# SwiGLU output products of three parts of four as seven block products for eight

## The chip, the cores and the metric

The kernel runs on one core of one Trainium2 chip. The metric is the device time of one execution in microseconds (us). Five engines are named: PE (TensorE) multiplies matrices and writes its sums into eight banks of PSUM; DVE (VectorE) and ACT (ScalarE) work element by element and read those banks; POOL (GpSimd) here issues transfers that add to what is in on-chip memory, and small copies; SP (SyncE) issues the plain transfers. Each engine takes its instructions in the order in which the program wrote them, and waits at one whose inputs are not there.

## The reference

Two layers of a decoder run over 544 tokens at once (512 of a prompt, 32 of eight samples), width 1024. Each layer has a SwiGLU feed-forward (FFN), a mixer and a second FFN, each added to the scaled input and normalised:

```python
def swiglu(x, w_in, w_out):
    g, u = jnp.split(x @ w_in, 2, axis=-1)
    return (jax.nn.silu(g) * u) @ w_out
...
x = layer_norm(ALPHA * x + 0.5 * swiglu(x, ffn1_w_in[layer], ffn1_w_out[layer]), ...)
```

`w_in` is 1024 x 5632 and `w_out` 2816 x 1024. There are four FFNs; the mixer of layer 0 is a retention with eight recurrent states of the samples per head, that of layer 1 a gated linear recurrence (RG-LRU). All in float32.

## The kernel before

**Precision and layout.** Activations lie transposed: 128 channels on the partitions, tokens along the row, in two halves of 272 tokens (`HF`). To multiply float32 values the kernel splits each operand into a high and a low part: ACT writes the high part (L314), DVE subtracts it from the source for the low part (L333), and a tile product is three matmuls (`mm3`, L372): high-high, high-low, low-high. `H`, the middle of the FFN, is 22 chunks of 128 channels; `Z` holds the sums that go to the normalisation; `X` is the split input.

**An FFN**, four times (`ffn`, L854), in this order: chunks 0 to 3 of H by plain products (the plain stage: 4 chunks, gate and up, two halves, 8 tiles, 3 matmuls: 384); then pairs of chunks (`pair`, L945), in which the two halves of tokens, the two halves of the 1024 inputs and the two chunks make 2 x 2 blocks, and seven block products stand for eight (Strassen and Winograd's way): 7 forms x 2 (gate, up) x 4 tiles x 3 = 168 matmuls. The forms of the weights (sums such as a21 + a22, called s1 to s4) are made by transfer: a block is loaded by SP (L489), another is added to it by POOL with an accumulating transfer (L477, `prev` and `more` in `use`, L416). The forms of X are made once per FFN (`sums`, L902). H is used in three parts, `PARTS = [(0, 8), (8, 16), (16, 22)]` (L36); after each part its product with `w_out` is done tile by tile (for 8 chunks: 8 outputs x 2 halves x 8 tiles x 3 = 384 matmuls), four outputs at a time (`gangs`), and DVE adds each bank to Z (`zev`, L699). With the last part the normalisation (`ln`, L621) begins.

**Supply of weights.** A unit is 128 x 1024 weights. It lands in one of 6 `raw` buffers (4 KB a partition; L48), is split by ACT and DVE (`split`, L447) into one of 6 `hl` buffers (8 KB; L49), and is freed by the last matmul that reads it. In the plain stage and in the RG-LRU two more hl buffers lie in unused working memory (`EXT`, L51, as `ext`); in pairs, output products and the retention there are none. A state of the retention keeps its raw buffer until the new state is stored (L515).

**Order.** Every instruction stream is written at build time by a small model of the engines (`Flow`): generators `yield` a time or an event, and are resumed when the modelled PE clock reaches it. Units are split in the order in which they were registered (`units`), and loaded in that order, with those that need an added block moved two places ahead (`order_loads`, `AHEAD`). The order of the instructions of each engine is thus fixed before the run; on the chip only semaphores wait.

## Time and profile before

| | |
|---|---|
| times of three runs | 2315.94, 2313.86, 2316.83 us; median 2315.94 |
| the profiled execution | 2316.85 us, of which the span (first to last instruction) 2315.1 |
| PE | 2273.5 us busy (98%), 17530 matmuls |
| DVE | 1540.3 us (67%) |
| ACT | 999.2 us (43%) |
| POOL | 143.7 us (6%) |
| transfers | 312.30 MB, mean 135 GB/s |
| mean granted PE clock | 0.992 |

Stages in us from the start of the span, by the outputs of PE and the loads: FFN 0 to 382, retention to 930, FFN to 1311, FFN to 1695, RG-LRU to 1937, FFN to the end. A row of the view by windows has: the stretch, its length, then the busy us (and the count of instructions) of PE, PEld (the loading of weights into PE), DVE, ACT and POOL, the granted clock of PE, the busy share of the 16 transfer engines, and GB/s. A row of the view by groups has: line, engine, operation, output <- inputs, shapes, count | busy us in total, mean ns of one | idle time of the engine before them and what ended it. A row of the timeline or of the chain of waits begins with the start and the length in us. An instruction's duration holds the way through its engine, so that two in a row overlap a little.

### The profile page before, as it was taken

To read this page: it belongs to the slowest core of one execution; us is meant where nothing else is said; L and a number is where in the kernel's file an instruction comes from. 1 tells how busy PE (TensorE), PEld (TensorE's weight loads), DVE (VectorE), ACT (ScalarE), POOL (GpSimd) and SP (SyncE) were. 2 spreads that over 40 slices of the span, in tenths; PEclk is the share of its full clock that TensorE was granted. 3 is DMA by queue.
4 is the path that set the end of the run, shared out by engine and by line. 5 is a ranking of instruction groups with operands and counts; after the bars stand their busy time and mean duration, and the time that the engine had idled before them with its cause. 6 is when DMAs were issued, how large, how long until landed. Compare 5 with 4: busy or idle time off the path is not lost.

```text
span 2315.1 us, 41946 instructions
## 1 busy us (share of the span) xinstructions
PE 2273.5 (98%) x17530; PEld 2230.4 (96%) x17530; DVE 1540.3 (67%) x2731; ACT 999.2 (43%) x1564; POOL 143.7 (6%) x195
## 2 busy tenths in 40 slices
PE   9999999999999999999999999999999999999997
PEld 9999998989899998999999899999989999999996
DVE  6646468776666677864746875564787678646467
ACT  5424244442434334542424453443458845424243
POOL 0011000000000000001100000101001000110000
PEclk9999999999999999999999999999999999999998
DMA  7666562153352543376756346665512232756651
GB/s 219 179 142 171 132 180 80 55 173 124 120 176 94 174 142 127 90 184 135 182 130 174 99 99 167 155 173 128 137 63 88 91 111 78 196 122 174 143 146 39
DMA packets 89486, 312.30 MB, mean 135 GB/s; under 512 B 9760, under 2 KB 13856, under 8 KB 89296
## 3 DMA queue, kind: packets, MB, share of 16 engines
q1 hardware_dynamic: 68016, 232.06, 30.5%
q0 software_dynamic: 21280, 77.56, 19.1%
q8 instruction: 137, 2.24, 0.4%
q14 instruction: 53, 0.43, 0.1%
HBM read 288.29 MB, written 21.29 MB: 134 GB/s over the span
## 4 chain that ended last, share of the span: by engine, by line
PE 91%; DVE 4%; issue 3%; ACT 1%; DMA 1%; SPq 0%; POOL 0%; ACTq 0%; POOLq 0%; DVEq 0%
PE bank L372 90%; PE bank L376 1%; DMA raw<-in_win 1%; DVE Z L333 1%; ACT ARF L314 0%; DVE ARF L342 0%; DVE Z L337 0%; DVE hl L333 0%; DVE ARF L333 0%; ACT hl L314 0%; DVE SM L351 0%; PE bank L380 0%; DVE ARF L337 0%; ACT Z L314 0%; DMA Z<-in_x 0%
## 5 line engine op out<-in xcount | busy, mean ns | idle before, releaser
L372 PE MATMUL bank<-BIG,hl 128*128 128x272 f32 x15096 | 1936.1, 290 | 16.7 <-ACT BIG L314 10.2
L372 PEld LDWEIGHTS bank<-BIG,hl 128*128 128x128 f32 x15096 | 1915.2, 189 | 28.9 <-ACT BIG L314 11.7
L333 DVE TENSOR_TENSOR hl<-raw,hl 128x1024 fp32r<-128x1024 f32 (+1 forms) x490 | 595.8, 1220 | 433.0 <-ACT hl L314 428.7
L314 ACT ACTIVATE hl<-raw 128x1024 fp32r<-128x1024 f32 (+1 forms) x490 | 511.8, 1054 | 661.3 <-PE bank L372 488.8
L314 ACT ACTIVATE BIG<-ARF 128x544 fp32r<-128x544 f32 (+11 forms) x234 | 131.1, 571 | 305.0 <-DVE ARF L337 219.5
L333 DVE TENSOR_TENSOR BIG<-ARF,BIG 128x544 fp32r<-128x544 f32 (+10 forms) x234 | 142.3, 618 | 110.2 <-ACT BIG L314 109.7
L477 POOL DMA_DIRECT2D raw<-in_win x144 | 125.2, 897 | 1395.6 <-DVE hl L333 749.0
L333 DVE TENSOR_TENSOR ARF<-bank,ARF 128x272 f32<-128x272 f32 (+3 forms) x460 | 187.0, 435 | 24.4 <-PE bank L372 16.6
L372 PE MATMUL bank<-BIG 128*128 128x272 f32 (+5 forms) x1172 | 193.7, 316 | 0.2 <-DVE ARF L342 0.2
L372 PEld LDWEIGHTS bank<-BIG 128*128 128x128 f32 (+3 forms) x1172 | 167.7, 188 | 13.7 <-DVE ARF L342 0.7
L372 PE MATMUL bank<-hl,BIG 128*128 128x256 f32 (+2 forms) x1024 | 145.7, 298 | 4.7 <-ACT BIG L314 4.2
L333 DVE TENSOR_TENSOR Z<-Z,bank 128x272 f32<-128x272 f32 (+1 forms) x230 | 110.5, 491 | 58.4 <-PE bank L372 53.7
L314 ACT ACTIVATE ARF<-bank 128x272 f32<-128x272 f32 (+5 forms) x278 | 108.8, 400 | 80.9 <-PE bank L372 51.3
L372 PEld LDWEIGHTS bank<-hl,BIG 128*128 128x128 f32 (+1 forms) x1024 | 126.4, 178 | 16.1 <-ACT BIG L314 4.6
L314 ACT ACTIVATE ARF<-Z 128x272 f32<-128x272 f32 (+1 forms) x86 | 39.3, 458 | 101.2 <-DVE Z L333 99.9
L333 DVE TENSOR_TENSOR ARF<-ARF 128x272 f32<-128x272 f32 (+1 forms) x146 | 61.2, 445 | 3.0 <-ACT ARF L314 1.4
L314 ACT ACTIVATE BIG<-Z,PR 128x272 fp32r<-128x272 f32 x80 | 40.8, 521 | 40.6 <-DVE Z L337 40.6
L314 ACT ACTIVATE ARF<-ARF 128x272 f32<-128x272 f32 x114 | 54.6, 492 | 3.6 <-DVE ARF L333 3.1
L337 DVE SCALAR_TENSOR_TENSOR Z<-Z,bank 128x272 f32<-128x272 f32 x80 | 33.5, 432 | 31.6 <-PE bank L372 31.4
L337 DVE SCALAR_TENSOR_TENSOR ARF<-ARF,PR 128x512 f32<-128x512 f32 (+1 forms) x92 | 40.5, 496 | 14.7 <-ACT ARF L314 14.7
L337 DVE SCALAR_TENSOR_TENSOR ARF<-ARF 128x272 f32<-128x272 f32 x84 | 46.7, 556 | 0.4
L337 DVE SCALAR_TENSOR_TENSOR raw<-raw,bank 128x512 f32<-128x512 f32 x64 | 40.9, 681 | 8.4 <-PE bank L372 8.3
(85 smaller groups left out, 653.2 us busy)
## 6 DMA issues: line engine op xcount, KB each, us to landing
raw<-in_win SPq DMA_DIRECT2D x173, 512.0 KB, 4.0
raw<-in_win POOLq DMA_DIRECT2D x144, 512.0 KB, 5.6
raw<-in_wout SPq DMA_DIRECT2D x88, 512.0 KB, 4.6
raw<-in_sret SPq DMA_DIRECT2D x32, 512.0 KB, 3.7
out_rets<-raw SPq DMA_DIRECT2D x32, 512.0 KB, 4.5
raw<-in_rwin_v SPq DMA_DIRECT2D x16, 512.0 KB, 3.6
raw<-in_rwin_kq SPq DMA_DIRECT2D x16, 512.0 KB, 3.7
raw<-in_rwin_g SPq DMA_DIRECT2D x16, 512.0 KB, 4.4
```

The lines of the kernel that those rows point to most:

```text
L314: nc.scalar.activation(out=out, in_=in_, func=func, scale=scale, **kw)
L333: nc.vector.tensor_tensor(out=out, in0=a, in1=b, op=op)
L337: nc.vector.scalar_tensor_tensor(out=out, in0=a, scalar=s, in1=b, op0=op0, op1=op1)
L372: nc.tensor.matmul(out, lhsT=a, rhs=b, start=start, stop=stop, skip_group_check=cont)
L376: nc.tensor.matmul(out, lhsT=a, rhs=b, start=start, stop=stop)
L477: nc.gpsimd.dma_start(out=u["raw"], in_=ap, accum_op=ALU.add)
```

## The change

The parts of H become `(0, 6), (6, 12), (12, 16), (16, 22)`. For the first three, the product with `w_out` is also done by seven block products: the 2 x 2 blocks are the two halves of tokens, the even and odd chunk of each pair of H, and two outputs out of four (`quad`: two per part, each 4 outputs). A quad of a part of 6 has 7 x 2 x 3 x 3 = 126 matmuls of 272 tokens, one of the part of 4 has 84. The fourth part stays tile by tile. For the quads the split forms of H (b11, b21, b22, n1, n3, nt, n4) are written by `put` and `mixed` at the end of each pair, and by `plain_forms` for chunks 0 to 3; their weights come in blocks of 768 or 512 columns, made into forms by the same loads and accumulating transfers. The seven forms, of pairs too, run in another order (`SEVEN`), and the banks of a quad are added to Z after every form. The order of the units changes with it. There are 5 raw and 5 hl buffers in place of 6 and 6; the memory goes into working memory that holds the forms of H, and the `ext` buffers become three in the plain stage and in the RG-LRU, and two in the last part of an FFN and in the retention. What is left out of the diff: the lines that go out of `pair`, the middle of `seven` (the three matmuls of each tile), the renamed `ext` arguments of the mixers, lengths of a unit in `split` and `pump`, and the signs in `sums`.

```diff
-PARTS = [(0, 8), (8, 16), (16, 22)]
-FH = 8
+PARTS = [(0, 6), (6, 12), (12, 16), (16, 22)]
+FH = 6
...
-N_RAW = 6
-N_HL = 6
-EXT = (10880, 12928, 8704, 13056)
+N_RAW = 5
+N_HL = 5
+EXT_R, EXT_S, EXT_M = (0, 1, 2), (3, 4, 5), (6, 7)
...
+    SEVEN = (("a11", 0), ("a12", 1), ("s2", 0), ("s3", 2), ("s1", 0), ("a22", 2), ("s4", 0))
...
+        res, last = [], None
+        for key, dram, n0, n in items:
+            blk = {f"a{r + 1}{c + 1}": dram[n0 + 2 * r + c] for r in range(2) for c in range(2)}
...
+            reg("s1", blk["a21"], more=blk["a22"])
+            if last:
+                last()
+            reg("a11", blk["a11"])
+            reg("a12", blk["a12"])
+            reg("s2", blk["a11"], prev=us["s1"])
+            reg("s3", blk["a21"], prev=us["a11"])
+            reg("a22", blk["a22"])
+            last = lambda reg=reg, blk=blk, us=us: reg("s4", blk["a12"], prev=us["s2"])
...
+    def seven(key, us, nk, moving, ev):
+        banks_of = {}
+        for form, bk in SEVEN:
+            u, mv = us[form], moving(form)
+            for i in range(2):
+                start = (bk, i) not in banks_of
+                if start:
+                    banks_of[bk, i] = acq_main()
+                else:
+                    fl.need(("rd", key, form, i))
...
+        def hforms(name, kk, n=1):
+            b = 6528 + 14 * HF * kk + ("b11", "b21", "b22", "n1", "n3", "nt", "n4").index(name) * 2 * HF
+            a = ARR[:, b:b + 2 * n * HF].rearrange("p (f a n) -> p a f n", a=2, n=HF)
+            return a[:, 0], a[:, 1]
+        def put(j, names, src, t):
+            hi, low = hforms(names[0], (j - PARTS[part_of[j]][0]) // 2, len(names))
+            t = act(hi, src, dep=t)
+            t = tt(low, src, f(hi), ALU.subtract, dep=t)
+            for name in names:
+                fl.set(("hs", nin, j, name), t)
+            return t
+        def mixed(j, b11, b12, b21, b22, N, t):
+            t = tt(N[:, 0], b11, b12, ALU.subtract, dep=t)
+            stt(N[:, 2], N[:, 0], -1.0, b22, ALU.mult, ALU.subtract)
+            t = tt(N[:, 3], b21, N[:, 2], ALU.add)
+            t1 = tt(N[:, 1], b12, b22, ALU.subtract)
+            put(j, ("nt", "n4"), N[:, 2:4], t)
+            return put(j, ("n1", "n3"), N[:, 0:2], t1)
...
+        def plain_forms(j):
+            h = HT[j // 2]
+            for i in (0, 1, 2, 3):
+                yield ("ht", nin, j + i % 2, i // 2)
+            yield ("sumd", g)
+            put(j, ("b11",), h[:, 0:1], 0.0)
+            put(j, ("b21", "b22"), h[:, 2:4], 0.0)
+            n = ar(lo + 8 * HF, 4, HF) if j == 0 else SG
+            t = mixed(j, h[:, 0], h[:, 1], h[:, 2], h[:, 3], n, 0.0)
+            fl.set(("hf", nin, j), t)
...
+        def pair(j, us, p):
...
                 if form == "a11":
+                    yield ("hf", nin, j - 4)
+                    t = act(a0[i], b, dep=t)
+                    fl.set(("rd", key, "s2", i), t)
+                elif form == "a12":
+                    yield ("rd", key, "s2", i)
+                    t = tt(a0[i], b, a0[i], ALU.add, dep=t)
+                    fl.set(("c11", key, i), t)
+                elif form == "s2":
+                    yield ("hf", nin, j - 2)
+                    t = act(q21[i], b, dep=t)
+                    fl.set(("rd", key, "s1", i), t)
+                elif form == "s3":
+                    yield ("hf", nin, j - 2)
+                    t = act(q22[i], b, dep=t)
+                    fl.set(("rd", key, "a22", i), t)
                 elif form == "s1":
+                    yield ("rd", key, "a22", i)
+                    t = tt(q22[i], q22[i], b, ALU.subtract, dep=t)
+                    fl.set(("rd", key, "s4", i), t)
+                    fl.set(("c22", key, i), t)
                 elif form == "a22":
+                    yield ("rd", key, "s1", i)
+                    t = tt(q21[i], b, q21[i], ALU.subtract, dep=t)
+                    fl.set(("c21", key, i), t)
+                elif not i:
+                    t = act(q12[0], b, dep=t, func=AF.Silu)
+                    fl.set(("c12", key, 0), t)
                 else:
+                    yield ("c12", key, 0)
+                    t = stt(q12[1], b, 0.5, q12[0], ALU.mult, ALU.mult, dep=t)
+                    fl.set(("c12", key, 1), t)
                 return t
...
+                plain = p == last_p
+                yield ("c11", key, 0)
+                ts = act(a0[0], a0[0], dep=fl.ev["c11", key, 0], func=AF.Silu)
+                yield ("c11", key, 1)
+                t = stt(a0[1], a0[1], 0.5, a0[0], ALU.mult, ALU.mult, dep=ts)
+                if plain:
+                    whole(0, a0[1], 0, t)
+                else:
+                    put(j, ("b11",), a0[1].unsqueeze(1), t)
+                for k in ("c22", "c21"):
+                    yield (k, key, 0)
+                ts = act(Q[:, 0, 0:TOK], Q[:, 0, 0:TOK], dep=fl.ev["c21", key, 0], func=AF.Silu)
+                for k in ("c22", "c21"):
+                    yield (k, key, 1)
+                t = stt(Q[:, 1, 0:TOK], Q[:, 1, 0:TOK], 0.5, Q[:, 0, 0:TOK], ALU.mult, ALU.mult, dep=ts)
+                if plain:
+                    whole(0, Q[:, 1, 0:TOK], 1, t)
+                else:
+                    put(j, ("b21", "b22"), Q[:, 1, 0:TOK].rearrange("p (f n) -> p f n", f=2), t)
+                yield ("c12", key, 1)
+                t = fl.ev["c12", key, 1]
+                if plain:
+                    t = whole(1, q12[1], 0, t)
+                else:
+                    t = mixed(j, a0[1], q12[1], q21[1], q22[1], N, t)
...
+        def quad(q, us, p):
...
+                def into(c, half, op, fresh=False):
+                    z = Z[:, m + c, hs(half)]
+                    if fresh and p == 0:
+                        return stt(z, z, ALPHA, b, ALU.mult, op, dep=t)
+                    return tt(z, z, b, op, dep=t)
+                def out(c, half, t):
+                    if p == last_p - 1:
+                        fl.set(("zp", g + 1, m + c, half), t)
+                if form == "a11":
+                    t = into(0, 0, ALU.add, True)
+                    fl.set(("rd", key, "s2", i), t)
+                elif form == "a12":
+                    yield ("rd", key, "s2", i)
+                    t = into(0, 0, ALU.add)
+                    out(0, 0, t)
+                elif form == "s2":
+                    t = into(1, 0, ALU.subtract, True)
+                    fl.set(("rd", key, "s1", i), t)
+                elif form == "s3":
+                    t = into(1, 1, ALU.add, True)
+                    fl.set(("rd", key, "a22", i), t)
+                elif form == "s1":
+                    yield ("rd", key, "a22", i)
+                    t = into(1, 1, ALU.subtract)
+                    fl.set(("rd", key, "s4", i), t)
+                    out(1, 1, t)
+                elif form == "a22":
+                    yield ("rd", key, "s1", i)
+                    t = into(1, 0, ALU.add)
+                    out(1, 0, t)
+                else:
+                    t = into(0, 1, ALU.add, True)
+                    out(0, 1, t)
+                return t
+            prog.append(lambda: seven(key, us, (j1 - j0) // 2, hmoving, ev))
...
+        items, runs = [], []
+        for p, (j0, j1) in enumerate(PARTS):
+            for j in range(max(j0, NE), j1, 2):
+                items.append(((nin, "pair", j), win, 2 * NE + 2 * (j - NE), 2 * HK))
+                runs.append(lambda us, j=j, p=p: pair(j, us, p))
+            if p < last_p:
+                for q in range(KC // 4):
+                    items.append(((nout, p, q), wout[p], 4 * q, j1 - j0))
+                    runs.append(lambda us, q=q, p=p: quad(q, us, p))
+                    if p == last_p - 1 and q:
+                        runs[-1] = lambda us, run=runs[-1]: (run(us), do(lambda: st.update(ext=EXT_M)))
+                    if p == 0 and not q and extra:
+                        runs[-1] = lambda us, run=runs[-1]: (do(extra), run(us))
+        for us, run in zip(seven_units(items), runs):
+            run(us)
...
+                n = j1 - j0
+                if p < len(PARTS) - 1:
+                    t = wo[j0:j1].reshape(n // 2, 2, 2, 2, 2, P, P).transpose(2, 4, 1, 5, 3, 0, 6)
+                    A[f"wout{w}{l}{p}"] = np.ascontiguousarray(t.reshape(8, P, n * P))
+                else:
+                    A[f"wout{w}{l}{p}"] = pack_tiles(wo[j0:j1].transpose(1, 0, 2, 3).reshape(-1, P, P))
```

More of the change, by code (lines that the diff above doesn't have):

```diff
@@ L452, in split @@
         cut = u.setdefault("cut", 1)
-        parts = [slice(i * UW // cut, (i + 1) * UW // cut) for i in range(cut)]
+        parts = [slice(i * u["w"] // cut, (i + 1) * u["w"] // cut) for i in range(cut)]
         t = max(u["t_raw"], t_hl + 0.1)
@@ L475, in add_block @@
     def add_block(u, ap, t):
-        nc.gpsimd.dma_start(out=u["raw"], in_=ap, accum_op=ALU.add)
-        st["dma"] = max(st["dma"], t + 1.5, fl.pe + 1.5) + 2.0
+        nc.gpsimd.dma_start(out=u["raw"][:, 0:u["w"]], in_=ap, accum_op=ALU.add)
+        st["dma"] = max(st["dma"], t + 1.5, fl.pe + 1.5) + 2.0 * u["w"] / UW
         u["t_raw"] = st["dma"] + 1.2
@@ L852, in build, with seven_units, reg, done @@
     cnt = {"sg": 0}
+    SEVEN = (("a11", 0), ("a12", 1), ("s2", 0), ("s3", 2), ("s1", 0), ("a22", 2), ("s4", 0))
+    def seven_units(items):
+        res, last = [], None
+        for key, dram, n0, n in items:
+            blk = {f"a{r + 1}{c + 1}": dram[n0 + 2 * r + c] for r in range(2) for c in range(2)}
+            us = {}
+            def reg(form, ap, key=key, us=us, n=n, **kw):
+                us[form] = use((*key, form), ap, n, **kw)
+            reg("s1", blk["a21"], more=blk["a22"])
[7 more added lines that the diff above has]
+            last = lambda reg=reg, blk=blk, us=us: reg("s4", blk["a12"], prev=us["s2"])
+            res.append(us)
+        last()
+        return res
+    def seven(key, us, nk, moving, ev):
[8 more added lines that the diff above has]
+                    fl.need(("rd", key, form, i))
+                b = banks_of[bk, i]
+                for k in range(nk):
+                    need_unit(u)
+                    xh, xl, e = mv(k)
+                    fl.need(e)
+                    off = (nk * i + k) * P
+                    wt = u["hl"]
+                    mm3(b[:, :HF], wt[:, 0, off:off + P], wt[:, 1, off:off + P], xh, xl, start and k == 0, k == nk - 1, not start)
+                    used(u)
+                    fl.poll()
+                def done(form=form, i=i, b=b, t=fl.pe + 0.1):
+                    t = yield from ev(form, i, b[:, :HF], t)
+                    if form in ("a12", "s4", "a22"):
+                        release(b, t)
+                fl.spawn(done())
     def ffn(l, w, g, final=False, extra=None):
@@ L932, in sums @@
             yield pace()
-            t = minus(T[:, 0], b21, HK, T[:, 2])
+            t = each(T[:, 0], b21, HK, T[:, 2], ALU.add, ALU.add)
+            fl.set(("sumd", g), t)
             yield ("plain", nin)
@@ L1040, in pair @@
-            prog.append(run)
-        def pair_units(js):
-            res = []
-            last = None
-            for j in js:
-                n0 = 2 * NE + 2 * (j - NE)
-                blk = {"a11": n0, "a12": n0 + 1, "a21": n0 + 2, "a22": n0 + 3}
-                us = {}
-                def reg(form, key=j, us=us, **kw):
-                    us[form] = use((nin, "pair", key, form), n=2 * HK, **kw)
-                reg("s1", ap=win[blk["a21"]], more=win[blk["a22"]])
-                if last:
-                    last()
-                reg("a11", ap=win[blk["a11"]])
-                reg("s2", ap=win[blk["a11"]], prev=us["s1"])
-                reg("a12", ap=win[blk["a12"]])
-                reg("s3", ap=win[blk["a21"]], prev=us["a11"])
-                reg("s4", ap=win[blk["a12"]], prev=us["s2"])
-                last = lambda reg=reg, blk=blk: reg("a22", ap=win[blk["a22"]])
-                res.append((j, us))
-            last()
-            return res
@@ new lines, in run, with hmoving, mv, ev @@
+                seven(key, us, HK, moving, ev)
+            prog.append(run)
+        def quad(q, us, p):
+            j0, j1 = PARTS[p]
+            key = (nout, p, q)
+            def hmoving(form):
+                name = {"a11": "b11", "a12": "b21", "s1": "n1", "s2": "nt", "s3": "n3", "a22": "n4", "s4": "b22"}[form]
+                def mv(k):
+                    hi, low = hforms(name, k)
+                    return hi[:, 0], low[:, 0], ("hs", nin, j0 + 2 * k, name)
+                return mv
+            def ev(form, i, b, t):
+                m = 4 * q + 2 * i
+                yield t
+                def into(c, half, op, fresh=False):
[31 more added lines that the diff above has]
+                    out(0, 1, t)
+                return t
+            prog.append(lambda: seven(key, us, (j1 - j0) // 2, hmoving, ev))
@@ new lines, in ffn, with gu @@
+        do(lambda: st.update(ext=EXT_S))
+        do(lambda: fl.spawn(sums()))
+        def gu(j, half):
+            return [lambda: job(wtiles(nin, win, (2 * j) * KC, range(KC), EXT_S), xrhs(g), half, ev_g(j, half)),
+                    lambda: job(wtiles(nin, win, (2 * j + 1) * KC, range(KC), EXT_S), xrhs(g), half, ev_u(j, half))]
+        do(lambda: [fl.spawn(plain_forms(j)) for j in range(0, NE, 2)])
+        for half in range(2):
+            gangs([x for j in range(NE) for x in gu(j, half)], FGA if g else 1)
@@ new lines, in ffn, with rhs @@
+        for us, run in zip(seven_units(items), runs):
+            run(us)
+        j0, j1 = PARTS[last_p]
+        n = j1 - j0
+        jobs = []
+        for m, half in ab(list(range(KC)), 7 if final else 4):
+            def rhs(k, half, j0=j0):
+                return H[:, 0, k, hs(half)], H[:, 1, k, hs(half)], ("h", nin, j0 + k, half)
+            jobs.append(lambda m=m, half=half: job(wtiles(nout + "l", wout[last_p], m * n, range(n), EXT_M), rhs, half,
+                                                   zev(m, half, False, True, (li, g + 1, final), count, guard)))
@@ L1094, in retention @@
+        gangs(jobs, 4)
     def retention(g):
```

181 lines of the change are left out of this document (47 added, 134 removed).

## The prediction

> **What bounds the kernel now.** I read the engines' busy times, then the chain of waits in order of time, then windows over the FFN of 1311 to 1695 us.
>
> ```profile
> span 2315.1 us, 41946 instructions
> PE 2273.5 (98%) x17530; PEld 2230.4 (96%) x17530; DVE 1540.3 (67%) x2731; ACT 999.2 (43%) x1564; POOL 143.7 (6%) x195
> PE 91%; DVE 4%; issue 3%; ACT 1%; DMA 1%; SPq 0%; POOL 0%; ACTq 0%; POOLq 0%; DVEq 0%
> ```
>
> PE is busy nearly always, but its matmuls overlap, so the chain says more. Two of its pieces are almost whole FFNs:
>
> ```profile
> 1330.02 333.11 PE bank L372 x2649
> 1937.04 331.18 PE bank L372 x2634
> ```
>
> Each matmul of 272 tokens takes 333.11 / 2649 = 0.1257 us (331.18 / 2634 gives the same), with no other engine in the chain for 330 us. So an FFN goes at the pace of PE: a matmul saved there is 0.1257 us as long as the other engines keep up. Windows (PE, PEld, DVE, ACT, POOL, clock, transfers) show their room:
>
> ```profile
> 1310.00:1330.00 20.00, 15.12 (x97) 14.23 (x97) 18.99 (x39) 10.24 (x19) 0.87 (x1) 0.83 0.42 109
> 1346.00:1367.00 21.00, 21.00 (x170) 21.00 (x169) 14.16 (x26) 10.65 (x19) 1.73 (x2) 1.00 0.29 51
> 1388.00:1409.00 21.00, 21.00 (x170) 21.00 (x169) 15.05 (x21) 11.01 (x15) 0.87 (x1) 1.00 0.73 209
> 1430.00:1457.00 27.00, 27.00 (x217) 27.00 (x216) 10.74 (x16) 4.24 (x4) 3.49 (x4) 1.00 0.62 135
> ```
>
> The first is the normalisation and the start of the next FFN; then the plain stage, pairs (1388), and an output product (1430), where DVE is busy only 10.7 of 27 us. The change takes PE work out of just that slack stage and puts DVE work in.
>
> **The change part by part.**
>
> *Removed from PE.* Of 16 of 22 chunks an output product has 16 x 8 x 2 x 3 = 768 matmuls; seven for eight leaves 672. That is 96 per FFN, 384 in all: 384 x 0.1257 = **48.3 us**. A quad of a part of 6 then takes 126 x 0.1257 = 15.8 us, one of the part of 4 takes 84 x 0.1257 = 10.6, a pair 168 x 0.1257 = 21.1. Pairs keep their count; only their order changes.
>
> *Added to DVE.* Its prices:
>
> ```profile
> L333 DVE TENSOR_TENSOR hl<-raw,hl 128x1024 fp32r<-128x1024 f32 x488 | 594.4, 1222 | 430.0 <-ACT hl L314 425.7 <-PE bank L372 2.9
> L333 DVE TENSOR_TENSOR BIG<-ARF,BIG 128x512 fp32r<-128x512 f32 x20 | 13.8, 692 | 14.0 <-ACT BIG L314 14.0
> L333 DVE TENSOR_TENSOR BIG<-ARF,BIG 128x544 fp32r<-128x544 f32 x98 | 70.0, 724 | 57.7 <-ACT BIG L314 57.7
> L333 DVE TENSOR_TENSOR Z<-Z,bank 128x272 f32<-128x272 f32 x182 | 76.3, 432 | 53.7 <-PE bank L372 53.7
> 1397.09 1.13 DVE L333 TENSOR_TENSOR ARF<-bank,ARF 128x272 f32<-128x272 f32 x3
> ```
>
> Three of 272 in a row take 1.13 us, so each after the first costs (1.13 - 0.43) / 2 = 0.35: about 0.08 less than its duration. By that a low part of 1024 costs 1.14, of 768 (between 544 and 1024) 0.88, of 544 0.64, of 512 0.61. A quad of 6 needs 7 low parts of weights and 14 additions to Z: 7 x 0.88 + 14 x 0.35 = 11.1 of 15.8 us (70%). A quad of 4: 7 x 0.61 + 4.9 = 9.2 of 10.6 (87%). A pair: 7 x 1.14 + 7 x 0.35 for banks + 4.7 at its end (six of 272, four of 544) = 15.1 of 21.1 (72%). Over 9 pairs and 6 quads of an FFN, some 190 of 275 us: on average PE still sets the pace.
>
> Around the part of 4 it is close. From its first quad's start to its second's end PE needs 21.1 us. DVE must do in it 28 additions (9.8), some 10 low parts (the other 4 can be ahead, as 5 buffers allow; 6.1) and what the last pair leaves (3.3): 19.2. The next pair's first three low parts (3.4) make it 22.6, and DVE has gaps in each stage, as the wait for ACT in the first row above shows (425.7 us in all). I take 1.25 us late per FFN, **+5**; ends 0 and +12 (all three of those low parts late every time).
>
> *Hand-over from a pair to its quads.* The third form of the first quad needs nt of that pair. The chain after the pair's last matmul: a product on DVE, then three of 272 (`mixed`), then ACT and DVE at 544. Hops between engines are short:
>
> ```profile
> 1409.42 0.43 DVE L337 SCALAR_TENSOR_TENSOR ARF<-ARF 128x272 f32<-128x272 f32 x1
> 1409.89 0.66 ACT L314 ACTIVATE BIG<-ARF 128x544 fp32r<-128x544 f32 x1 [2.02 <-DVE ARF L337]
> 1410.58 0.73 DVE L333 TENSOR_TENSOR BIG<-ARF,BIG 128x544 fp32r<-128x544 f32 x1 [0.72 <-ACT BIG L314]
> ```
>
> 0.43 + 0.43 + 2 x 0.35 + 0.66 + 0.73 + four hops of 0.04 = 3.1 us, and a low part queued ahead on DVE adds up to 1.1. PE has until then a11, a12 and the first chunks of s2: 42 matmuls (5.3 us) with 6 chunks, 27 (3.4) with 4. In order on DVE behind this chain stand the additions of a11, for whose bank PE waits next. I take 0.5 us at four hand-overs and 0.25 at eight, **+4**; ends 0 and +12 (1 us at each).
>
> *Plain stage to the first pair.* `plain_forms` drops 8 low parts of 272 per FFN and adds per two chunks one of 272, three of 544 and four of 272: 2 x 3.7 - 2.8 = +4.5 us of DVE, most of it after the last plain products, in a pair that has 6 us of slack; in the same pair DVE forms a22 of X. The pair's bank for s2 is emptied only after `plain_forms` has ended. **+3**; ends 0 and +10.
>
> *Fewer buffers.* In pairs 5 hl buffers, one held by s1 while four other forms run, leave a lead of three forms (9 us in a pair, 4.5 in a quad of 4), more than ACT 0.7 + DVE 0.7. In the retention hl rises from 6 to 7 and raw falls from 6 to 5, where states hold raw:
>
> ```profile
> 379.61 0.33 SPq L489 DMA_DIRECT2D raw<-in_sret  x1
> 467.28 0.35 SPq L515 DMA_DIRECT2D out_rets<-raw  x1
> 382.00:930.00 548.00, 535.85 (x3884) 502.93 (x3883) 393.41 (x803) 217.72 (x385) 3.06 (x5) 0.99 0.40 129
> ```
>
> The first state waits 88 us for its store, and four lie there by then, leaving one buffer in place of two, with SP's queue in order behind it. PE idles 12 us there now, so the ends are -5 and +12; I take **+2**. The RG-LRU keeps 8 hl.
>
> *Added transfers.* A quad moves 8 blocks, four of them by POOL with addition, at the same bytes per matmul as a pair. That a packet of 2 or 3 KB costs less than one of 4 KB is seen at the output of y, of packets of about 1 KB (rows of the whole run, then of 2290 to 2315.1):
>
> ```profile
> q1 hardware_dynamic: 68016, 232.06, 30.5%
> q0 software_dynamic: 21280, 77.56, 19.1%
> q1 hardware_dynamic: 2192, 2.23, 25.4%
> ```
>
> 0.305 x 2315 x 16 / 68016 = 166 ns a packet against 0.254 x 25.1 x 16 / 2192 = 47; an adding one takes 332. At cost by bytes a quad loads the engines as a pair does (0.73 above). If adding packets cost 332 at any size, a quad of 4 needs 4 x 128 x (85 + 332) / 16 = 13.3 us against 10.6: 2.8 late, eight times, 22 us. I take 0, since plain packets follow their bytes. Latency is tighter (POOL's adding transfers, 512 KB, from issue to landing):
>
> ```profile
> DMA to landing us min/median/max: 5.0/5.6/9.6
> ```
>
> In a quad of 4 the chain a11 split, a21 added, s3 split, then three more splits before the next a11 takes 5.6 + 0.63 (ACT, by its rows near that of 544) + 0.7 + 4 x 0.61 + 0.4 of hops = 9.8 of 10.6 us at the latency of 512 KB; proportional to bytes it is 7.0. At 9.6, the longest, it is 13.8 and PE waits. I add nothing for it beyond the 5 above.
>
> [...]
>
> **Sum.** -48.3 + 5 + 4 + 3 + 2 = -34.3. Against the profiled execution, 2316.85 (0.9 above the median of three runs): **2282.5**, said as 2282.
>
> **The rivals.**
>
> *All hidden.* The lead of three forms takes up every lag, as the 330-us pieces without a break do today: 2316.85 - 48.3 = 2268.6; with the retention at its good end 2264. Against it: DVE at 107% around the part of 4.
>
> *Late weights.* Adding transfers land toward the long end of their row when the engines are loaded, and the in-order splits stop behind them: 3 us at each of the eight small quads rather than 1.25 per FFN: 2282.5 - 5 + 24 = 2301. For: 13.8 against 10.6 at the longest landing; against: the median.
>
> *Slower: PE waits for its banks in the quads.* Each quad goes back to a bank eight times, each only after DVE has added it to Z, and 24 quads give 192 such waits. DVE is in order, and a low part that waits for ACT or a landing holds the addition behind it; PE has three groups of matmuls (2.3 us at 4 chunks, 3.4 at 6) to hide it. At a mean loss of 0.25 us (48.3 / 192) the gain is gone. Each low part of the whole run waits, where it waits,
>
> ```profile
> DVE hl L333 <- ACT hl L314: 428.7, 307, 6.2
> ```
>
> 1.4 us; an addition caught behind one with its 1.1 us and a second low part is 3.6 late. If that loses 0.7 at each of 64 waits in small quads and 0.3 at 128 in large ones: 45 + 38 = 83, so 2316.85 - 48.3 + 83 = 2352. Against it: pairs have the same eight returns at 72% of DVE and show no break.
>
> [...]
>
> **How the numbers follow.** Forecast (2274 to 2292): 0.50. All hidden: 0.20. Late weights or more of the same (2292 to 2311): 0.14. Middle cases within 0.2% (2311 to 2321; about what a measurement of this kernel can tell from no change): 0.05. Slower: 0.11. So faster 0.84. The range leaves out the slower cases, the middle ones and the ends beyond: 2265 to 2306. That the products are not fewer can't be: the forms are written out.
>
> **What would show it.** Of the changed kernel: PE 17530 - 384 = 17146 matmuls. Low parts of 768 and 512 columns at about 0.95 and 0.69 us. POOL with 96 more transfers. Windows on the quads of 4: DVE above 85%, PE with small gaps after them; on the quads of 6: none. PE waiting for Z (DVE) in the table of waits: under 15 us in all for the forecast, near 80 for the slower rival. PE held by hl from the transfers: the late weights. The retention within -5 and +12 of 548 us. I am wrong if PE's gaps in the FFNs add up to over 25 us, or if a stage outside the FFNs moves by over 12.

## The result: slower by 2.6%

The changed kernel takes 2375.74 us (median; 2373.13 to 2377.8) against 2316.22 us (2313.86 to 2316.83) before: a ratio of 1.0258, 95% interval 1.0241 to 1.0276. The forecast was 2282.

From the page of the changed kernel: span, busy times, queues, and the two rows of the chain's shares.

```profile
span 2375.6 us, 42241 instructions
PE 2263.2 (95%) x17146; PEld 2208.6 (93%) x17146; DVE 1708.2 (72%) x3087; ACT 1126.2 (47%) x1871; POOL 229.7 (10%) x291
...
q1 hardware_dynamic: 72624, 232.06, 28.9%
q0 software_dynamic: 35104, 111.12, 26.8%
...
PE 63%; DMA 12%; issue 12%; DVE 8%; ACT 4%; POOL 1%; SPq 0%; ACTq 0%; POOLq 0%; DVEq 0%
```

PE has the 384 matmuls less that it was to have, but its busy time fell by 10.3 us and not by 48.3, and its idle time (span less busy) rose from 41.6 to 112.4: 70.8 - 10.3 = the 60.5 us between the two spans. The missing 38 us of busy time are matmuls at a lower clock, mostly: the view of cores has a mean granted clock of 0.980 (before 0.992), and 2.0% of 2375.6 less 0.8% of 2315.1 is 29 us.

```profile
core 0: 2375.6 us, clock 0.980
```

By the last normalisation's matmuls the four FFNs take 13.2, 18.5, 20.0 and 15.4 us longer than before (where they took 400.6, 381.9, 380.0 and 378.7), the retention 5.1 and the RG-LRU 1.6 less. So the whole loss is in the FFNs, where each was to win 12.1.

The 330-us pieces of PE in the chain of waits are gone (the longest now within one FFN is 73.5 us). What stands between is in the table of waits (us in total, times, longest). `BIG` holds the split activations, `ARF` is the working memory into which the banks of a pair are emptied, `raw` and `hl` are weights before and after their split. First before, for PE and ACT, then the changed kernel:

```profile
PE bank L372 <- ACT BIG L314: 14.3, 6, 4.2
...
ACT hl L314 <- DMA raw<-in_win: 85.3, 36, 5.9
```

```profile
PE bank L374 <- ACT BIG L316: 27.3, 16, 4.2
PE bank L374 <- DVE Z L335: 25.7, 12, 5.9
PE bank L374 <- ACT ARF L316: 24.5, 20, 3.0
PE bank L374 <- DVE Z L339: 9.3, 4, 3.4
...
ACT hl L316 <- DMA raw<-in_win: 94.9, 39, 4.6
```

Before, PE waited 14.3 us for `BIG` on ACT and 1.7 at most in any one row for Z. Now it waits for additions to Z on DVE (35 us) and for ACT to empty banks (`ARF`, 24.5 us). ACT itself waits for landings of `w_in` not much longer than before (94.9 us against 85.3), when PE hardly waited; for landings of `w_out` it waits 47.0 us more. One wait of PE, in order of time, at the end of the quads of a part of 6 in the third FFN:

```profile
1536.29 0.86 POOL L479 DMA_DIRECT2D raw<-in_wout  x1 [1.84 <-DVE hl L335]
1538.23 10.85 SPq L491 DMA_DIRECT2D raw<-in_win  x3
...
1545.67 2.52 ACT L316 ACTIVATE hl<-raw 128x768 fp32r<-128x768 f32 x3 [6.18 <-DMA raw<-in_wout]
1546.55 0.96 DVE L335 TENSOR_TENSOR hl<-raw,hl 128x768 fp32r<-128x768 f32 x1 [5.02 <-ACT hl L316]
1547.42 0.43 DVE L335 TENSOR_TENSOR Z<-Z,bank 128x272 f32<-128x272 f32 x1
...
1548.00 1.24 PE L374 MATMUL bank<-BIG,hl 128*128 128x272 f32 x8 [2.55 <-DVE Z L335]
```

Read it from the end. PE stood 2.55 us for a Z addition of 0.43 us. The addition stood on DVE behind a low part of weights, which waited 5.02 us for ACT, which waited 6.18 us for a block that an adding transfer brought, issued at 1536.29. That late block is of form s3. PE was only about to begin s2, whose weights ACT had split at 1538.65; what it lacked was the bank, from which a11 had not yet been added to Z. Windows over the same stretch (busy time of PE, PEld, DVE, ACT, POOL, then clock, share of the DMA engines, GB/s) show what the DMA engines did before and what the clock did behind it:

```profile
1536.00:1546.00 10.00, 9.45 (x76) 9.23 (x74) 4.34 (x9) 2.02 (x3) 1.73 (x2) 1.00 1.03 232
1546.00:1556.00 10.00, 8.00 (x51) 8.03 (x52) 7.05 (x12) 4.10 (x5) 1.75 (x2) 0.83 0.67 155
```

The engines were full (1.03). In the second window PE was busy for 8 us and did 51 matmuls, which at 0.1257 take 6.4.

The issues with their sizes and median landing:

```profile
raw<-in_win SPq DMA_DIRECT2D x173, 512.0 KB, 5.1
raw<-in_win POOLq DMA_DIRECT2D x144, 512.0 KB, 7.6
raw<-in_wout SPq DMA_DIRECT2D x64, 384.0 KB, 3.9
raw<-in_wout POOLq DMA_DIRECT2D x64, 384.0 KB, 5.5
...
raw<-in_wout POOLq DMA_DIRECT2D x32, 256.0 KB, 5.8
```

An adding transfer of 512 KB, those of the pairs, landed after 5.6 us before and after 7.6 now, a plain one after 4.0 and 5.1. The adding transfers of the quads themselves took 5.5 and 5.8 us in the median; the one above took 9.3.

### The profile page after: what moved, and what is told of

Same layout as the page of the kernel before. It is cut to its first block, busy times and chain, and to the rows that moved or that the text cites. A ratio compares the mean times of both kernels' runs of the same rounds, so it can differ in the third digit from the quotient of the medians.

```text
span 2375.6 us, 42241 instructions
## 1 busy us (share of the span) xinstructions
PE 2263.2 (95%) x17146; PEld 2208.6 (93%) x17146; DVE 1708.2 (72%) x3087; ACT 1126.2 (47%) x1871; POOL 229.7 (10%) x291
## 4 chain that ended last, share of the span: by engine, by line
PE 63%; DMA 12%; issue 12%; DVE 8%; ACT 4%; POOL 1%; SPq 0%; ACTq 0%; POOLq 0%; DVEq 0%
PE bank L374 61%; DMA raw<-in_win 9%; DMA raw<-in_wout 4%; ACT hl L316 2%; DVE hl L335 2%; DVE ARF L335 1%; DVE Z L335 1%; PE bank L378 1%; POOL raw L479 1%; DVE Z L339 1%; ACT ARF L316 1%; DVE BIG L335 1%; ACT BIG L316 1%; DVE ARF L339 1%; DVE BIG L339 0%
## 5 line engine op out<-in xcount | busy, mean ns | idle before, releaser
L374 PE MATMUL bank<-BIG,hl 128*128 128x272 f32 x13224 | 1736.8, 293 | 92.3 <-DVE Z L335 25.7
L374 PEld LDWEIGHTS bank<-BIG,hl 128*128 128x128 f32 x13224 | 1705.7, 192 | 114.2 <-ACT ARF L316 29.2
L335 DVE TENSOR_TENSOR hl<-raw,hl 128x1024 fp32r<-128x1024 f32 (+2 forms) x555 | 614.9, 1112 | 353.7 <-ACT hl L316 347.4
L316 ACT ACTIVATE hl<-raw 128x1024 fp32r<-128x1024 f32 (+2 forms) x555 | 530.5, 966 | 499.5 <-PE bank L374 298.1
L374 PE MATMUL bank<-BIG 128*128 128x272 f32 (+5 forms) x3108 | 441.9, 298 | 0.4 <-DVE ARF L344 0.4
L374 PEld LDWEIGHTS bank<-BIG 128*128 128x128 f32 (+2 forms) x3108 | 413.0, 187 | 17.2 <-DVE ARF L344 0.8
L316 ACT ACTIVATE ARF<-bank 128x272 f32<-128x272 f32 (+4 forms) x422 | 160.4, 394 | 128.1 <-PE bank L374 80.3
L335 DVE TENSOR_TENSOR Z<-Z,bank 128x272 f32<-128x272 f32 (+1 forms) x438 | 190.8, 461 | 34.2 <-PE bank L374 26.5
L479 POOL DMA_DIRECT2D raw<-in_wout x96 | 86.0, 919 | 478.8 <-DVE hl L335 320.6
L335 DVE TENSOR_TENSOR ARF<-bank,ARF 128x272 f32<-128x272 f32 (+3 forms) x244 | 103.5, 438 | 29.8 <-PE bank L374 20.0
```

Source lines behind the costliest of these rows:

```text
L316: nc.scalar.activation(out=out, in_=in_, func=func, scale=scale, **kw)
L335: nc.vector.tensor_tensor(out=out, in0=a, in1=b, op=op)
L374: nc.tensor.matmul(out, lhsT=a, rhs=b, start=start, stop=stop, skip_group_check=cont)
L479: nc.gpsimd.dma_start(out=u["raw"][:, 0:u["w"]], in_=ap, accum_op=ALU.add)
```

## Experiments

Three theories stood at the start. A: adding transfers land later than the planner's price says, and ACT, DVE and PE stop behind them in order. B: the smaller sets of buffers (5 raw, 5 hl). C: work on DVE at the hand-over from pair to quad and around the bank additions. The first four runs tell these apart.

**pairs_5_5** is the kernel before with 5 raw and 5 hl in pairs and outputs; the freed space serves elsewhere.

```diff
-N_RAW = 6
-N_HL = 6
+N_RAW = 5
+N_HL = 5
+    SPARE = sbt("spare", 2, UW, dt=F32R)
```

> The kernel before (2316 us), its products and order of forms unchanged, but with 5 raw buffers everywhere and 5 hl buffers in pairs and in the first two output products (elsewhere a sixth as before). Theory A (late adding transfers in the added block products hold ACT, DVE and so PE): 2316, at most 2326. Theory B (too few buffers cause the loss of the change, in pairs too): 2340 or more. Theory C (the work of the hand-over and of the bank additions on DVE causes it): 2316, as A.

2318.41 us (2316.62 to 2320.7), ratio to before 1.0005 (0.9996 to 1.0014). B falls for pairs and for products tile by tile; in quads fewer buffers have no run of their own.

**tiles_new_order** is the changed kernel with its order of the seven, its parts and buffers, but every output product tile by tile.

```diff
-                plain = p == last_p
+                plain = True
...
+                jobs.append(lambda m=m, half=half, p=p, n=n, rhs=rhs:
+                            job(wtiles(nout + str(p), wout[p], m * n, range(n), EXT_M), rhs, half,
+                                zev(m, half, p == 0, p == last_p, (li, g + 1, final), count, guard)))
```

> The changed kernel (2376 us) with all output products tile by tile again: parts of 6, 6, 4, 6, the new order of the seven forms in pairs, 5 raw and 5 hl. 384 matmuls more than the changed kernel, so 48.3 us more of PE. A: the loss goes with the block products: about 2312 (the 5 us that the retention gained stay). B, or the new order as the cause: 2340 or more. C: as A.

2302.04 us (2301.72 to 2303.13), 0.9936 (0.9921 to 0.9951). So the block products alone cost 73.7 us over this base, where 48.3 fewer us of matmuls were to be had. The base itself beats before; its waits of PE for `BIG` are 3.1 us against 14.3, because the three waits of 4.16 us at the normalisations behind the first three FFNs (at 387, 1315 and 1696 us of before) aren't there: one of 1.9 us is left. No run tested why. A had said about 2312.

**quad_no_add** leaves out the sums of the output products' weight blocks: the blocks are loaded plainly, so the products are not the reference's.

```diff
+            if key[0][:3] == "out":
+                reg("s1", blk["a21"])
...
+                for form, block in (("a11", "a11"), ("a12", "a12"), ("s2", "a11"), ("s3", "a21"), ("a22", "a22")):
+                    reg(form, blk[block])
```

> The changed kernel, but in the added block products each of the seven weight blocks is a plain load of one block: the sums of weight blocks there are left out. Same matmuls, same ACT and DVE work, 96 adding transfers fewer, 72 plain loads more. A: most of the waits behind late splits go: 2376 - 60 = 2316, between 2295 and 2335. B: buffers are as few as before: within 15 of 2376. C: ACT and DVE work is unchanged: within 10 of 2376.

2320.99 us (2315.15 to 2328.43), 1.0018 (1.0005 to 1.0032): 54.8 us of the loss are gone with the 96 added transfers (there are 72 more plain loads in their place).

**later_splits** leaves the work alone and changes three prices in the planner, so that it issues the splits later in ACT's list.

```diff
-        st["dma"] = max(st["dma"], t + 1.5, fl.pe + 1.5) + 2.0 * u["w"] / UW
-        u["t_raw"] = st["dma"] + 1.2
+        st["dma"] = max(st["dma"], t + 1.5, fl.pe + 1.5) + 2.7 * u["w"] / UW
+        u["t_raw"] = st["dma"] + 3.0
...
-            t = st["dma"] + 0.9
+            t = st["dma"] + 1.9
```

> The changed kernel, with the planner told that transfers land later (adding ones 2.7 us of engine time and 3.0 us to land in place of 2.0 and 1.2, plain ones 1.0 us later), so that it writes the splits later into the streams of ACT and DVE, behind bank additions that it wrote behind them before. Nothing else changes. A: fewer additions stand behind a late split: 2340, between 2320 and 2360. B: splits start later still with few buffers: 2376 or more. C: within 10 of 2376.

2323.23 us (2319.72 to 2327.38), 1.0023 (1.0013 to 1.0033): 52.5 us come back by order alone, within A's ranges in this run and the one above. C, which had both within 10 us of 2376, falls as the main cause. The waits of PE for additions and emptied banks, and ACT's for landings, in later_splits:

```profile
PE bank L374 <- DVE Z L335: 5.6, 4, 3.8
PE bank L374 <- DVE Z L339: 2.4, 2, 2.1
PE bank L374 <- ACT ARF L316: 1.9, 4, 0.5
...
ACT hl L316 <- DMA raw<-in_win: 21.7, 17, 2.6
```

The three rows of PE were 59.5 us and are 9.9. The transfers are as late as they were (medians of 7.2 us at 512 KB and 6.0 at 384). Which of the three prices matters was not tried. Two controls followed. **later_splits_no_add** has the plain loads of quad_no_add (so it too leaves out the sums of weight blocks) on top of these prices, **tiles_later_splits** has the prices in tiles_new_order.

> later_splits (2323.2 us) with the sums of the output products' weight blocks left out: these blocks are loaded plainly, so the products are not the reference's; all else as in later_splits. Theory A: in later_splits the adding transfers of the part of 4 still hold ScalarE 0.5 to 2.5 us at several block products, about 6 us in each of four layers: 2300 us. If the planner's later prices have hidden all adding transfers already and only hand-over and rates are left (theory C): 2321 us, as in the run quad_no_add.

> tiles_new_order (2302.0 us: all output products tile by tile) with the three changed prices of later_splits in the planner: adding transfers 2.7 us per full row and 3.0 us to land, plain ones 1.9 us to land. Theory A (the changed prices help because they keep late adding transfers from holding up ScalarE in the block products, which this kernel doesn't have): 2302 us, 5 us to either side. Rival (the prices help any kernel with adding transfers, in the pairs too): 2290 us or less.

The first took 2323.5 us (2319.32 to 2325.54): with the later prices the adding transfers cost nothing any more; A had expected 2300 here and was wrong on that; C had 2321. The second took 2304.85 us (2302.77 to 2305.96): the prices do nothing for a kernel without quads. So the loss of 52 to 55 us needs both, late transfers and splits that are issued too early for them; either taken away, it is gone.

**What is left in later_splits**, some 55 us above 2268.6. Its waits of PE:

```profile
PE bank L374 <- ACT BIG L316: 25.0, 14, 4.2
```

Two are the 4.16 at normalisations, one of 1.91 is at another, one of 0.27 at the start; the other ten, 14.5 us, are hand-overs (of 12). One such, with DVE's list ahead of it, from the changed kernel's timeline (the two `...` leave out ACT's rows and the rest of the chain):

```profile
1414.79 0.43 DVE L339 SCALAR_TENSOR_TENSOR ARF<-bank,ARF 128x272 f32<-128x272 f32 x1
1415.14 0.43 DVE L339 SCALAR_TENSOR_TENSOR Z<-Z,bank 128x272 f32<-128x272 f32 x1
...
1416.05 0.96 DVE L335 TENSOR_TENSOR hl<-raw,hl 128x768 fp32r<-128x768 f32 x1 [0.48 <-ACT hl L316]
1416.93 0.43 DVE L339 SCALAR_TENSOR_TENSOR Z<-Z,bank 128x272 f32<-128x272 f32 x1
1417.27 0.43 DVE L335 TENSOR_TENSOR ARF<-ARF 128x272 f32<-128x272 f32 x1
...
1419.40 0.39 PE L374 MATMUL bank<-BIG,hl 128*128 128x272 f32 x1 [1.18 <-ACT BIG L316]
1420.16 1.52 PE L374 MATMUL bank<-BIG,hl 128*128 128x272 f32 x10 [0.37 <-DVE BIG L335]
```

c12 is done at 1415.22 (the first row), and `mixed` begins at 1417.27, behind two additions and a low part. **handover_at_once** issues it straight behind c12 and makes nt ahead of n4; **rates_spread** lets in the small operations of the RG-LRU constants one by one (they had held an addition in the third FFN, at 1406 us, where PE waited 3.80 us; the expectation calls it the fourth); **handover_and_rates** does both.

```diff
             t = tt(N[:, 0], b11, b12, ALU.subtract, dep=t)
...
-            put(j, ("nt", "n4"), N[:, 2:4], t)
+            put(j, ("nt",), N[:, 2:3], t)
+            put(j, ("n4",), N[:, 3:4], t2)
...
+                    if ("fin", key) in fl.ev:
+                        fl.set(("hf", nin, j), mixed(j, a0[1], q12[1], q21[1], q22[1], N, t))
...
             act(e, lam, func=AF.Abs)
+            yield fl.pe + 0.5
             act(e, e, func=AF.Exp, scale=-1.0)
```

> later_splits (2323.2 us) with one edit: the mixed sums of a pair (nt, n4, n1, n3) are issued straight behind the last product c12, ahead of the weights' low parts and the additions to Z that stood before them on VectorE, and nt is split off and put first. Theory C (the residue is the hand-over from pair to quad: 12 times 1.18 to 1.83 us for SCALAR_TENSOR-made nt on ScalarE plus 0.37 us for its low part, because VectorE reached the mixed sums late): about 1.2 us each comes back, 14 us, 2309 us. Rival (the chain product, four VectorE operations, split, low part is itself longer than the two block products that cover it): 3 us at most, 2320 us. Theory A alone (late adding transfers are all of it): 2323 us.

> later_splits (2323.2 us) with the thirty small operations that make the RG-LRU constants let in one by one, 0.5 us apart, in place of all at once in front of the additions to Z of the first block products of the fourth feed-forward layer. There TensorE waits 3.80 us for an addition to Z and runs at a lower clock behind it. Theory C (a wait of PE for VectorE work in front of a bank's addition is paid in full): 4 to 6 us less, 2318 us. If the wait only moves to the next late transfer: 2323 us.

> Both edits of the two runs beside it. Theory C: the gains add, 19 us, 2304 us. If what bounds the stage is the weights' adding transfers (theory A), the time saved at the hand-over is lost again at the next split of weights: 2315 us or more.

2316.29 (2310.12 to 2320.5), 2321.14 (2316.81 to 2323.92) and 2311.87 us (2309.82 to 2313.41): 6.9, 2.1 and 11.4 us less than later_splits, together six tenths of what C had expected. The 2.1 alone are within the spread of the runs. In handover_at_once the ten waits at hand-overs are gone, but only half of their 14.5 us came back: PE's waits for additions to Z (both rows) rose from 8.0 to 27.8. Windows over quads of 6 (1387 and 1484) and of 4 (1560) in handover_and_rates, then over output products in tiles_new_order, show the next suspect:

```profile
1387.00:1420.00 33.00, 30.42 (x233) 29.51 (x234) 26.88 (x70) 13.16 (x17) 6.97 (x8) 1.00 0.82 189
1484.00:1517.00 33.00, 31.87 (x253) 31.43 (x252) 25.92 (x47) 13.96 (x18) 6.96 (x8) 1.00 0.83 193
1560.00:1582.00 22.00, 19.02 (x134) 18.45 (x134) 17.20 (x38) 8.35 (x14) 4.35 (x5) 0.92 0.70 180
```

```profile
1383.00:1420.00 37.00, 37.00 (x296) 37.00 (x296) 19.26 (x52) 11.98 (x15) 2.59 (x3) 1.00 0.50 112
1484.00:1521.00 37.00, 37.00 (x297) 37.00 (x296) 15.98 (x25) 9.93 (x12) 2.59 (x3) 1.00 0.48 110
```

DVE is busy 78 to 81% in quads, 43 to 52% tile by tile. Theory E: that is the bound. D: only its order is. G: the part of 4 is too short to cover its hand-overs of banks. **low_deferred** issues the low parts inside quads only when ACT is about done with the high part, so that additions pass them; **parts_6664** moves the part of 4 to the end; the third does both. All stand on handover_and_rates.

```diff
-            prog.append(lambda: seven(key, us, (j1 - j0) // 2, hmoving, ev))
+            prog.append(lambda: (st.update(defer=True), seven(key, us, (j1 - j0) // 2, hmoving, ev), st.update(defer=False)))
...
-PARTS = [(0, 6), (6, 12), (12, 16), (16, 22)]
+PARTS = [(0, 6), (6, 12), (12, 18), (18, 22)]
```

> handover_and_rates (2311.9 us) with one edit: inside the block products of the output, a weights' low part is issued on VectorE only when its split on ScalarE is about done, in place of right behind it in the list. What is left there are 8 us of waits of TensorE in each feed-forward layer, most of them named for an addition to Z, with some 10 us of lower clock in all. Theory D (the additions to Z stand behind low parts that wait for ScalarE, in order): additions pass, half of the waits go, 2296 us. Rival E (VectorE has too much work in these stages, the order doesn't matter): 2312 us. Rival F (the low parts are then late themselves and TensorE waits for weights): over 2315 us.

> handover_and_rates (2311.9 us) with the parts 6, 6, 6, 4 in place of 6, 6, 4, 6: three parts of six by block products, the part of four last and plain. 12 matmuls fewer in each of the four layers (6 us in all), and no block products with 12 matmuls a form. Theory G (the part of four is too short to cover its splits, 1.27 us of matmuls for each hand-over of a bank; 5 us of waits in each layer and a lower clock behind): 2312 - 6 - 20 = 2286 us. Rival E (VectorE's work in the block products is the bound, of six as of four): 2306 us or more.

> Both edits of the two runs beside it. If D and G name different waits they add: 2278 us. If they name the same ones: 2286 us. Rival E: 2306 us.

2336.48 us (2332.78 to 2338.57), 2313.73 (2310.45 to 2317.12) and 2322.71 (2321.07 to 2327.65). Theory D falls, as rival F said: in low_deferred PE waits for the weights themselves.

```profile
PE bank L374 <- ACT hl L316: 19.1, 10, 4.2
PE bank L374 <- DVE hl L335: 16.7, 23, 0.9
```

Neither work can be put first: the additions late cost a bank, the low parts late cost a weight. parts_6664 doesn't decide on G, since its products of four chunks at the end bring a wait of their own, at the normalisation's sums:

```profile
PE bank L378 <- DVE ARF L335: 17.4, 8, 3.5
```

The last four runs stand on handover_and_rates too. **short_additions** adds only 68 of 272 columns to Z in quads; **short_low_parts** forms a quarter of the columns of a quad's low weights; **short_both** does both. What is left out makes Z and the products other than the reference's; PE's work and the transfers stay.

```diff
-                    z = Z[:, m + c, hs(half)]
+                    z = Z[:, m + c, half * HF:half * HF + 68]
+                    b = bank[:, 0:68]
...
+                if u["key"][0][:3] == "out" and len(u["key"]) == 4:
+                    w = slice(w.start, w.start + (w.stop - w.start) // 4)
```

> handover_and_rates (2311.9 us) with the additions of the output's block products to Z cut to 68 of 272 columns, so that three quarters of these sums are left out and Z is not the reference's; TensorE's work and the weights are as before. VectorE stands at 79 to 81% in these stages, 43 to 52% where the same products are done tile by tile. Theory E (VectorE has too little slack there; TensorE waits for additions and low parts in turn): VectorE falls to about 58%, most of the 42 us of idle time and lower clock goes, 2280 us. Rival H (the waits come from ScalarE's splits and the weights' arrival, VectorE only passes them on): 2308 us. Rival I (the additions' own length of 0.43 us from a bank's last matmul to its next is what is paid): the gain is there too, and short_low_parts has none.

> handover_and_rates (2311.9 us) with the low parts of the weights of the output's block products cut to a quarter of their columns, 0.25 us in place of 0.95; the rest of the low weights is left out, so the products are not the reference's; all additions to Z in full. Theory E: VectorE falls to about 52%, 2280 us as with the short additions. Rival H: 2308 us. Rival I (the length of an addition itself): 2308 us here, 2280 with the short additions.

> Both cuts together (three quarters of the additions to Z and of the low weights are left out). Theory E: what is left is what the stages cost with VectorE near 30%; if VectorE is all of the rest, the 48 us of matmuls saved show against before, 2268 us. Rival H: over 2300 us.

2303.37 us (2298.56 to 2304.56), 2292.27 (2287.84 to 2295.8) and 2282.91 (2279.48 to 2293.26): 8.5, 19.6 and 29.0 us less, with the same work on ACT, PE and the transfers. Over the second quads of 6 in the third FFN in short_both, and over most of the first ones in short_low_parts, PE has no gap, at a DVE load of 45 and 69%, though the transfer engines are as busy as before:

```profile
1465.00:1492.90 27.90, 27.90 (x226) 27.90 (x225) 12.64 (x43) 11.70 (x14) 6.08 (x7) 1.00 0.90 216
```

```profile
1380.00:1413.00 33.00, 33.00 (x266) 33.00 (x265) 22.76 (x67) 15.58 (x20) 6.11 (x7) 1.00 0.95 223
```

So of the 43 us that handover_and_rates stands above 2268.6, 29 go with DVE's load in the quads (E), the low parts more than the additions. E had expected more: 2280 for each cut alone and 2268 for both. H, by which the waits come from ACT and the landings, falls, and so does I, by which the low parts would have brought nothing. One rival is left: the planner prices the shorter operations too and writes the lists anew (in short_both one in six of ACT's instructions stands at another place), so a part of the 29 us can be order. No run kept the lists and shortened the work.

**four_by_tiles** keeps the quads for the parts of 6 alone.

```diff
-                plain = p == last_p
+                plain = p >= last_p - 1
...
-            if p < last_p:
+            if p < last_p - 1:
```

> handover_and_rates (2311.9 us) with the part of four computed tile by tile again (192 matmuls a layer in place of 168) and block products for the two parts of six alone. In the profile the part of four has 5 us of idle time and one halved clock window in each layer for 3 us of matmuls saved. Theory G (the part of four's block products cost more than they save): 2312 + 12 - 28 = 2296 us. Rival (its waits move to the parts of six): 2320 us.

2289.39 us (2286.49 to 2291.22), 0.9873 (0.9857 to 0.9889): the best kernel of all, 28.6 us under the runs of before beside it (2317.98). Its busy times from the page, and the one row of its waits that shrank most against before (14.3 us there):

```profile
PE 2239.0 (98%) x17242; PEld 2191.7 (96%) x17242; DVE 1659.1 (73%) x2983; ACT 1112.9 (49%) x1849; POOL 202.0 (9%) x259
```

```profile
PE bank L374 <- ACT BIG L316: 2.1, 2, 1.9
```

Giving 96 matmuls back (12.1 us) won 22.5 us. Not all of that is the part of 4: the 4.16-us waits at the normalisations are gone here, as in tiles_new_order. In handover_and_rates they are two, with 6.4 and 4.9 us at clock 0.50 behind them, by an estimate from these figures 8.3 + 5.7 = 14 us. That leaves some 8 us for the part of 4 (G). Against tiles_new_order, which shares the shorter waits, the quads of 6 win 12.7 us of the 288 x 0.1257 = 36.2 that they save (15.5 against tiles_later_splits, which has the same prices).

## Why the prediction was wrong

Between 2268.6, the time with all hidden, and 2375.7 lie 107 us. In the order of the runs: 52.5 are late adding transfers with splits issued too early for them, 11.4 the hand-over and the RG-LRU constants, 29.0 go with DVE's load in the quads, 14.3 are open. The prediction had 14 for everything. Its sign of being wrong, PE's gaps in the FFNs above 25 us, came true: PE's idle time rose by 70.8.

*Removed from PE*: right. 17146 matmuls, and short_both's PE is busy 2229.0 us, 44.5 less than before.

*Added transfers*, "I take 0": this is the step that failed, by some 52 to 55 us. It put the chain at the median landing of before, 5.6 us, and named 9.6 as the case in which PE waits. For the quads' own transfers the median held (5.5 and 5.8), though the engines were full in places and single landings took over 9 us. What was argued from it held as well: no row of PE's waits in the changed kernel names weights. But lateness alone was not the price: in later_splits the adding transfers are about as late, and later_splits_no_add shows that they cost nothing. The price came from where the split stood in ACT's list. The planner counts an adding row as 2.0 us on the engines and 1.2 to land and puts the split there. The sum took the queue of splits as a lead that covers such lags, and gave no price to what stands behind a split that is issued too early: a low part on DVE, behind it the addition, behind that PE's bank.

The rivals *late weights* (0.14, 2301) and *PE waits for its banks* (0.11, 2352) were set up as two, each with half of the cause: the first stopped the splits and then only the weights were late, the second had the additions caught behind low parts, at a mean price for each wait. They were one chain, transfer, ACT, low part, addition, PE. The second named the right end of it and had 83 us for it, where the waits for additions and emptied banks came to 59.5 and the lower clock to some 29 more; the time lay 24 us above its 2352. "Pairs have the same eight returns at 72% of DVE and show no break" was the argument against it, and it didn't carry over to quads; why pairs bore it was not tried.

The cost by bytes was about right, at 0.225 us a packet against 0.197: (0.268 x 2375.6 - 0.191 x 2315.1) x 16 / 13824 added packets = 0.225, and 0.332 x 2428 / 4096 bytes = 0.197. The landing of adding transfers didn't go by their bytes here, as the chain's 7.0 us had it: in the changed kernel the median was 7.6 us at 512 KB, 5.5 at 384 and 5.8 at 256.

*DVE around the part of 4* (+5) and the loads of 70% and 87%: the shape was wrong. DVE has 79 to 81% in quads of 6 and 78% with gaps in quads of 4, and what goes with its load is 29 us in all quads, not 5 around one part. (The prediction's own prices add up to 199 us of 274 in an FFN's pairs and quads, not 190.) "On average PE still sets the pace" is true and no bound: each product hands over eight banks and seven weights to an engine that works in order.

*Hand-over* (+4, ends 0 and +12): mis-sized. PE waited 14.5 us at ten of the 12 hand-overs in later_splits; about 7 came back by order. The chain was counted with one low part ahead; two additions stood there too. The RG-LRU constants in the third FFN's first quad were missed: 2.1 us in one pair of runs and 4.4 in the other, the first not clear of the spread.

*Fewer buffers* (+2; -5 to +12): not a cost: pairs_5_5 is within 0.05% of before, and the retention is 5.1 us shorter, at the good end of the range. *Plain stage to the first pair* (+3) has no run of its own. The prices of low parts (0.95 and 0.69 us; measured 0.956 and 0.689) were right.

The sum has no price for PE's clock. It needed one: behind a wait of 2.05 us in handover_and_rates the clock was 0.50 (last section), and by the mean clocks of 0.980 and 0.992 the changed kernel lost some 29 us to it. What stays open: the 14 us between short_both and 2268.6 (a quarter of the additions and low parts is still there); against tiles_new_order less 48.3, 2253.7, it is 29 us, of which the two waits of 4.16 us are 8. Open too is how much of DVE's 29 us is order, and why the 4.16-us waits at the normalisations come and go with the order of the last tiles.

## What to carry to other kernels

Where engines work in order, ask of every added transfer not only when its data are needed but what is queued behind the instruction that waits for it, on every engine down to the one that sets the pace; a list written by a planner is only as good as its prices for the transfers. When work is taken from the bound engine and given to one with 50% load, the gain holds while that engine's worst stretch, not its mean, keeps up: here 36 us saved were worth some 13. If one block size doesn't cover its own overhead, try the change on the sizes that do.

## What the runs showed of the hardware

Behind one wait of PE of about 2 us the trace has its clock at 0.50, behind another of the same length at 1.00. Here are windows around two waits of 2.05 us each in handover_and_rates, one that ends at 1561.95 and one that ends at 1178.04:

```profile
1560.10:1563.50 3.40, 1.55 (x10) 1.40 (x11) 3.38 (x8) 1.64 (x4) 0.00 (x0) 1.00 0.24 55
1563.50:1566.90 3.40, 3.40 (x17) 3.40 (x16) 2.38 (x6) 0.83 (x2) 0.86 (x1) 0.50 0.90 245
1566.90:1570.30 3.40, 3.40 (x29) 3.40 (x29) 2.94 (x7) 1.49 (x3) 1.76 (x2) 1.00 0.44 100
```

```profile
1174.35:1177.76 3.41, 1.64 (x14) 1.42 (x12) 3.36 (x8) 2.93 (x6) 0.00 (x0) 1.00 0.08 13
1177.76:1181.18 3.42, 3.15 (x23) 2.99 (x24) 3.36 (x8) 0.70 (x2) 0.86 (x1) 1.00 0.69 217
```

Behind the first wait PE ran at clock 0.50 for 3.40 us, with 17 matmuls in place of the 29 of the row after it: 12 x 0.1257 = 1.5 us lost, an estimate from these rows. Behind the second, of which 0.28 us fall into its second row, the clock was 1.00. In the rows ahead PE was busy 1.55 and 1.64 us, but the busy time alone doesn't tell which it will be: in the changed kernel, around two waits of 1.18 and 0.37 us, a stretch with 1.87 us of PE has 0.50 behind it.

```profile
1125.88:1129.30 3.42, 1.87 (x13) 1.49 (x12) 3.02 (x7) 1.94 (x3) 0.00 (x0) 1.00 0.40 117
1129.30:1132.71 3.41, 3.41 (x17) 3.41 (x16) 2.93 (x6) 0.84 (x1) 1.76 (x2) 0.50 0.30 50
```

So of two waits of the same 2.05 us one cost 1.5 us more than the other. What decides between them was not shown.
